# Stick-breaking attention in a four-layer trunk: from keys on partitions and softplus sums to queries on partitions, sigmoids and a reversed scan

## The chip, the cores and the metric

The kernel runs on one core of one Trainium2 chip. The core's engines each work through a queue of their own: TensorE (PE; its weight loads are listed apart as PEld), VectorE (DVE), ScalarE (ACT), GpSimd (POOL) and SyncE (SP, which issues the loads). The metric is the device time of the whole program in microseconds (us), as the median of several runs. The trace comes from one more, profiled execution.

## The reference

A trunk of four layers over 512 tokens of width 1024. Each layer is a token mixer followed by a gated FFN. The four mixers are a Conformer convolution, HGRN2, mLSTM and, in the last layer, stick-breaking attention with 16 heads of 64. Only that last mixer is touched here. What it computes for one head, with q, k, v the three thirds of `h @ w_qkv`:

```
z[i, j]  = q[i] . k[j] / sqrt(64)
log_w[i, j] = log_sigmoid(z[i, j]) + sum over l in (j, i) of log_sigmoid(-z[i, l])     for j < i
A[i, j]  = exp(log_w[i, j])   for j < i,  else 0
o[i]     = sum over j of A[i, j] v[j]
out      = concat of heads @ w_out
```

In other words, key j takes the share sigmoid(z) of what the keys between it and the query have left over; a key l leaves the share sigmoid(-z).

## The kernel before

All matrices that carry weights are multiplied as three products of high and low parts (`hh` and `hl` of the activations, `wh` and `wl` of the weights, all in the fp32r format). A weight unit of 512 KB is loaded by SP into `raw` (three buffers), ScalarE casts it to the high part (L255) and VectorE subtracts to get the low part (L257); units of an output projection are first multiplied on VectorE by the row of gates (L245). `up` (L285) makes a projection with features on partitions: 8 blocks of the input times 3 products, 24 matmuls of 512 columns for 128 features. `down` (L354) makes a projection with tokens on partitions.

`stick` (from L1149) works on 8 pairs of heads, 128 features to a pair. First the values `sv` of all heads are made, tokens on partitions, in fp32. Then, for each pair `p`, nine steps:

- `queries` and `keys`: two `up` units, `p_sqk`. From PSUM each head gets three tiles of 128 rows in which the high part stands in one half of the rows and the low part in the other (`sq`, `sk`, and `sx` with the halves exchanged), so that one matmul over 128 rows sums two of the products. ScalarE and VectorE share this work (L1211 to L1224).
- `scores`, once per head: `z`, keys on partitions and queries on columns, two fp32r matmuls for each block row (L1236). Of the 4 by 4 blocks only the 10 on and above the diagonal are made: 1280 columns in the tile `zt`, which ScalarE copies out of PSUM (L1238).
- `softplus`, once per head: Abs, Exp and Ln on ScalarE (L1247 to L1249), a VectorE step (L1250), the strict triangle on the diagonal blocks (`stri`, L1252), and the split into `sh` (ScalarE, L1253) and `sl` (VectorE, L1254).
- `weigh`, once per head: the sum over later keys is a sum over partitions, so it is done with 20 fp32r matmuls against a triangle of minus ones, `negu`, and a full square of minus ones, `negone`, into three banks `c` (L1265). VectorE adds it to `zt` (L1271), ScalarE takes Exp (L1273), VectorE clears the masked half of the diagonal blocks (`smask`, L1276).
- `mix`: values times weights in fp32, head 0 into columns 0 to 63 of the array and head 1 into 64 to 127, one bank `so` (L1284); split into `soh` and `sol` (L1287, L1288).

The steps are emitted in an order set by the table `STEPS` (a step of pair p is emitted at p plus its number) and put in place on each engine by the scheduler. Behind the last pair comes the output projection `swo`, by `down` with three units early (`pe_swo`), then the rest and the last three units (TAIL) token block by token block, so that normalisation (`X`, statistics, L581 to L626), transposes (`tr`, L512) and the new `hh` and `hl` (L517 to L524) of one token block go on beside the matmuls of the next. The FFN behind it starts with `up_head`: half the columns of three units as soon as two token blocks are ready (`p_f`).

HGRN2 uses the same program parts at its own end, but with `down_late` instead of `down`: there the last phase has 12 matmuls for each token block.

## Time and profile before

| | us |
|---|---|
| median of 3 runs | 2760.55 (2756.59 to 2761.02) |
| the profiled execution | 2756.47 |
| its span in the trace | 2754.6 |
| PE busy over the span | 2655.6 (96%) |
| DVE busy | 2027.7 (74%) |
| ACT busy | 1270.9 (46%) |
| stick-breaking from the first `p_sqk` to the first `p_f` behind it | 2141.36 to 2376.97 |

The span is what the trace covers; the 1.9 us between it and the execution's own time lie around it. Shares of busy time are means over stages with different limits, so the stage that the diff touches is read by itself in the rows below. In every PE row the duration of one matmul runs from its issue to its modelled end and overlaps its neighbours; the distance between two starts is what a matmul costs the queue. An fp32 matmul stands as two instructions in the trace, an fp32r matmul as one. A row "x16" of a timeline is 16 instructions in a row of one group, its second figure the time from the first one's start to the last one's end.

### The profile page before, as it was taken

To read this page: it belongs to the slowest core of one execution; us is meant where nothing else is said; L and a number is where in the kernel's file an instruction comes from. 1 tells how busy PE (TensorE), PEld (TensorE's weight loads), DVE (VectorE), ACT (ScalarE), POOL (GpSimd) and SP (SyncE) were. 2 spreads that over 40 slices of the span, in tenths; PEclk is the share of its full clock that TensorE was granted. 3 is DMA by queue.
4 is the path that set the end of the run, shared out by engine and by line. 5 is a ranking of instruction groups with operands and counts; after the bars stand their busy time and mean duration, and the time that the engine had idled before them with its cause. 6 is when DMAs were issued, how large, how long until landed. Compare 5 with 4: busy or idle time off the path is not lost.

```text
span 2754.6 us, 33739 instructions
## 1 busy us (share of the span) xinstructions
PE 2655.6 (96%) x12980; PEld 2128.7 (77%) x12980; DVE 2027.7 (74%) x3133; ACT 1270.9 (46%) x1773; POOL 43.7 (2%) x80
## 2 busy tenths in 40 slices
PE   7979999999998999999999999999999999999998
PEld 5538888877776788887887777888887777888886
DVE  7558997674777699667756777997676688766676
ACT  3134433345674443334545444443334798543432
POOL 0000000000000000000000000000000000000000
PEclk9989999999999999999999999999999999999999
DMA  9844874222221386232222322873333211333222
GB/s 322 235 110 155 299 236 143 95 100 89 85 72 45 126 295 222 92 102 92 98 79 77 97 79 95 276 258 121 100 103 99 62 48 31 106 100 110 97 92 77
DMA packets 109673, 352.33 MB, mean 128 GB/s; under 512 B 12104, under 2 KB 22600, under 8 KB 109512
## 3 DMA queue, kind: packets, MB, share of 16 engines
q1 hardware_dynamic: 109512, 350.17, 38.5%
q8 instruction: 102, 1.67, 0.2%
q14 instruction: 59, 0.48, 0.1%
HBM read 341.63 MB, written 8.50 MB: 127 GB/s over the span
## 4 chain that ended last, share of the span: by engine, by line
PE 79%; DVE 9%; ACT 8%; DMA 2%; issue 2%; POOL 1%; SPq 0%; POOLq 0%; DVEq 0%; ACTq 0%
PE p_f L285 34%; PE p_d L354 16%; PE p_mup L285 5%; PE p_pw L285 3%; PE p_mdn L354 3%; PE p_hqf L285 2%; PE p_hv L354 1%; PE p_sv L354 1%; PE pc L683 1%; PE p_pw L354 1%; PE p_hg L285 1%; PE p_hwo L406 1%; PE ms L977 1%; PE tr L512 1%; ACT hf L517 1%
## 5 line engine op out<-in xcount | busy, mean ns | idle before, releaser
L285 PE MATMUL p_f<-hh,wh_f 128*128 128x512 f32 (+1 forms) x1504 | 565.4, 377 | 1.5 <-ACT hh L523 1.5
L285 PE MATMUL p_f<-hl,wh_f 128*128 128x512 f32 (+1 forms) x1504 | 566.5, 377 | 0.0
L285 PE MATMUL p_f<-hh,wl_f 128*128 128x512 f32 (+1 forms) x1504 | 565.6, 376 | 0.0
L255 ACT CAST wh_f<-r_f 128x1024 fp32r<-128x1024 f32 x176 | 185.2, 1054 | 345.1 <-PE p_f L285 310.1
L285 PEld LDWEIGHTS p_f<-hh,wh_f 128*128 128x128 f32 x1504 | 284.0, 189 | 53.1 <-ACT hh L523 1.8
L285 PEld LDWEIGHTS p_f<-hl,wh_f 128*128 128x128 f32 x1504 | 284.2, 189 | 51.1 <-issue 0.2
L285 PEld LDWEIGHTS p_f<-hh,wl_f 128*128 128x128 f32 x1504 | 284.1, 189 | 51.3 <-issue 0.2
L257 DVE TENSOR_TENSOR wl_f<-r_f,wh_f 128x1024 fp32r<-128x1024 f32 x176 | 215.1, 1224 | 133.8 <-ACT wh_f L255 133.1
L211 DVE CUSTOM_DVE_ANT_0 ada<-ada,sbc,adab 128x1024 f32<-128x1024 f32 x192 | 243.9, 1280 | 6.8 <-DMA ada<-in_ada_dram 6.8
L1331 DVE SCALAR_TENSOR_TENSOR cv<-p_f,par,cv 128x511 f32<-128x511 f32 (+1 forms) x176 | 131.4, 746 | 1.4
L1331 DVE SCALAR_TENSOR_TENSOR cg<-p_f,par,cg 128x511 f32<-128x511 f32 (+1 forms) x176 | 131.3, 746 | 1.3
L245 DVE TENSOR_TENSOR r_d<-r_d,gate 128x1024 f32<-128x1024 f32 x88 | 107.5, 1222 | 28.5 <-DMA r_d<-in_fdn_dram 27.7
L1341 ACT ACTIVATE cg<-cg 128x512 f32<-128x512 f32 x88 | 55.5, 630 | 154.9 <-DVE cg L1331 154.9
L257 DVE TENSOR_TENSOR wl_d<-r_d,wh_d 128x1024 fp32r<-128x1024 f32 x88 | 107.5, 1221 | 11.7 <-ACT wh_d L255 11.7
L285 PE MATMUL p_mup<-hh,wh_mup 128*128 128x512 f32 (+1 forms) x280 | 107.4, 384 | 0.9 <-ACT hf L517 0.9
L285 PE MATMUL p_mup<-hh,wl_mup 128*128 128x512 f32 (+1 forms) x280 | 106.3, 380 | 0.0
L285 PE MATMUL p_mup<-hl,wh_mup 128*128 128x512 f32 (+1 forms) x280 | 105.9, 378 | 0.0
L255 ACT CAST wh_d<-r_d 128x1024 fp32r<-128x1024 f32 x88 | 92.4, 1050 | 20.5 <-PE p_f L285 16.6
L626 ACT ACTIVATE X<-X,mv 128x512 f32<-128x512 f32 x56 | 43.0, 811 | 79.4 <-DVE mv L614 79.4
L1329 ACT ACTIVATE cg<-p_f,par 128x512 f32<-128x512 f32 x88 | 68.2, 774 | 13.2 <-PE p_f L285 13.2
L1329 ACT ACTIVATE cv<-p_f,par 128x512 f32<-128x512 f32 x88 | 68.1, 774 | 3.9 <-PE p_f L285 3.9
L354 PE MATMUL p_d<-wl_d,gr2h 128*128 128x512 f32 x176 | 69.6, 396 | 0.0
(510 smaller groups left out, 5868.0 us busy)
## 6 DMA issues: line engine op xcount, KB each, us to landing
ada<-in_ada_dram SPq DMA_DIRECT2D x192, 512.0 KB, 4.6
r_f<-in_fup_dram SPq DMA_DIRECT2D x176, 512.0 KB, 3.9
r_d<-in_fdn_dram SPq DMA_DIRECT2D x88, 512.0 KB, 3.3
r_mup<-in_mup_dram SPq DMA_DIRECT2D x32, 512.0 KB, 3.3
r_pw<-in_pw_dram SPq DMA_DIRECT2D x24, 512.0 KB, 7.5
r_hqf<-in_hqf_dram SPq DMA_DIRECT2D x16, 512.0 KB, 3.3
r_mdn<-in_mdn_dram SPq DMA_DIRECT2D x16, 512.0 KB, 3.3
r_sqk<-in_sqk_dram SPq DMA_DIRECT2D x16, 512.0 KB, 3.6
```

The costliest lines, as they stand in the source:

```text
L211: nc.vector.tensor_tensor_reduce(out=raw, in0=raw, in1=self.sbc, scale=1.0, scalar=ab[:, j:j + 1], op0=ALU.mult, op1=ALU.add, accum_out=ac ...
L245: nc.vector.tensor_tensor(out=r, in0=r, in1=gr, op=ALU.mult)
L255: nc.scalar.copy(hi, raw)
L257: nc.vector.tensor_tensor(out=lo, in0=raw, in1=hi.bitcast(F32), op=ALU.subtract)
L285: self.nc.tensor.matmul(ps[:, c0:c1], a, b[:, k, c0:c1], start=(n == 0), stop=(n == 3 * KD - 1))
L354: self.nc.tensor.matmul(bank, l[:, ts_], r, start=(kp == first and a == n == 0), stop=(kp == last and a == 1 and n == 2))
L406: self.nc.tensor.matmul(bank, l[:, ts_], r, start=(kp == first and a == n == 0), stop=(kp == last and a == 1 and n == 2))
L512: nc.tensor.transpose(ps[:, j * P:(j + 1) * P], n[:, k * P:(k + 1) * P], self.ident)
L626: nc.scalar.activation(out=o[:, hs], in_=x[:, hs], func=AF.Identity, scale=mv[:, 2:3], bias=mv[:, 3:4])
L1329: nc.scalar.activation(out=o, in_=ps, func=AF.Identity, scale=w[2], bias=par[:, C_CONVB + m:C_CONVB + m + 1])
L1331: nc.vector.scalar_tensor_tensor(out=o[:, s:], in0=ps[:, :T - s], scalar=w[2 - s], in1=o[:, s:], op0=ALU.mult, op1=ALU.add)
L1341: nc.scalar.activation(out=cg, in_=cg, func=AF.Silu)
```

## The change

Only `stick`, its constants and one argument of `down_late` differ.

- Scores stand with queries on partitions and keys on columns. `p_sqk` is evicted once, in plain fp32, by ScalarE (tiles `sq`, `sk`, both heads in one tile). Each head's 64 rows are one row group of the array, and its matmuls are plain fp32 over 64 rows; those of the two heads alternate, into two banks. The packing into `sq`, `sk`, `sx` is gone.
- ScalarE reads each score bank twice: sigmoid(-z) into `sg` and sigmoid(z) into `sb`. The columns of one head are in two parts: 512 (query block 3) and 768 (blocks 2, 0 and 1 as 384, 128, 256).
- VectorE runs one scan over each part of `sg`, in place and from the last column to the first (multiply by `sg`, then maximum with the constant `sown`, which is 1 at the end of each block's keys and so starts the product afresh). In the rows of DVE's order below the scan stands as SCALAR_TENSOR_TENSOR. Then `sb` is multiplied by `sg` moved by one column. Softplus, the split, the `c` matmuls and Exp are gone.
- The weights now stand with queries on partitions, and `mix` wants keys there: 20 transposes of 128 by 128 for each pair (`turn_a`, `turn_c`) into banks `at`. ScalarE copies the full blocks out and VectorE masks the diagonal ones on the way (`evict`), into `sa`.
- `values` multiplies 20 blocks of 128 columns, column groups as before, into the bank `so`.
- PE's order is written by hand: a list `todo` sorted by numbers in which a pair takes 2 units. Projections go in halves of 12 matmuls between the other steps of three pairs.
- `swo` goes through `down_late`: four units early, in eight chunks of 12 matmuls, in place of the projections behind the last pair; one unit as a bridge; then 18 matmuls for each token block.
- One table of activation functions (sigmoid) is taken in place of another (ln and exp).
- SP loads the constant `sown` (128 by 896) in place of `stri` and `negu`; nothing else changes in its order.

```diff
-STEPS = dict(q0=-1.69, k0=-0.87, z0=-0.6, z1=-0.39, s0=-0.19, w0=0.2, s1=0.3, w1=0.5, m0=1.13)
-ORD = (0, 1, 3, 2)
-ZTB, SPB, SHB, SLB = 4, 2, 1, 1
+BB, AB = (2, 3), (2, 2)
...
+    dg = (p_ <= f_).astype(np.float32)
+    o["sown"] = np.concatenate([dg * x for x in (0, 0, 0, 1, 1, 0, 1)], axis=1)
...
-        hls = [[load(h, kp) for kp in left[h]] for h in range(2)]
+        last = [(h, kp) for h in range(2) for kp in left[h]][-2:]
+        hls = [[load(h, kp, spare if (h, kp) in last else None) for kp in left[h]] for h in range(2)]
...
-            self.psum(mm="01", z="237", c="456")
+            self.psum(mm="01", z="234", t="56", o="7")
...
+            W = (T, 768)
+            cols = (((3, 0),), ((2, 0), (0, 384)), ((1, 512),))
+            masks = (own[:, 0:T], own[:, P:7 * P])
...
+            def project(u, dst, half):
+                if half == 0:
...
+                    self.up_mm(st["pq"], st["hl"], 0, T, range(4))
+                    return
+                self.up_mm(st["pq"], st["hl"], 0, T, range(4, KD))
...
+                nc.scalar.copy(z, st["pq"])
...
+            def scores(p, g):
...
+                for b, c in cols[g]:
+                    w = (b + 1) * P
+                    for hh in range(2):
+                        r = slice(HD * hh, HD * hh + HD)
+                        nc.tensor.matmul(zb[hh][:, c - c0:c - c0 + w], q[r, b * P:(b + 1) * P], k[r, 0:w], start=True, stop=True,
+                                         tile_position=(HD * hh, 0))
+                    n = c - c0 + w
                 for hh in range(2):
...
+                    for name, sc in (("g", -1.0), ("b", 1.0)):
+                        nc.scalar.activation(out=st[name, p, part][hh][:, c0:c0 + n], in_=zb[hh][:, 0:n], func=AF.Sigmoid,
+                                             scale=sc * HD ** -0.5)
...
+                    nc.vector.tensor_tensor_scan(out=G[:, ::-1], data0=G[:, ::-1], data1=masks[part][:, ::-1], initial=1.0,
+                                                 op0=ALU.mult, op1=ALU.max)
+                    nc.vector.tensor_tensor(out=B[:, 0:w - 1], in0=B[:, 0:w - 1], in1=G[:, 1:w], op=ALU.mult)
+
+            def evict(ps, dst, lo, hi, dg):
+
+                nc.scalar.copy(dst[:, lo:hi], ps[:, lo:hi])
...
+                                        in1=smask.rearrange("p (a c) -> p a c", a=1).broadcast_to([P, m, P]), op=ALU.bitwise_and)
...
+                    for x in range(4):
+                        nc.tensor.transpose(ps[:, x * P:(x + 1) * P], st["b", p, part][hh][:, x * P:(x + 1) * P], self.ident)
+                    evict(ps, a[hh], 0, (384, 256)[part], (384, 256)[part])
...
+            dn = self.down_late(ins["swo"], KD, lambda k, h: so[k], "swo", done, [(1, (0, 1)), (0, (0, 1))], (2,), gate=gate,
+                                spare=lambda tag, nm: late["p"].tile([P, D], F32R, tag="tw", bufs=4, name=nm))
+            todo = []
+            for p in range(KD):
+                for z, u in (("q", p), ("k", KD + p)):
+                    for half in range(2):
+                        todo.append((2 * p + (z == "k") + half / 2, lambda u=u, d=(z, p), half=half: project(u, d, half)))
+                for at, fn in ((2.4, lambda p=p: scores(p, 0)), (2.9, lambda p=p: scores(p, 1)), (3.4, lambda p=p: scores(p, 2)),
+                               (4.4, lambda p=p: turn_a(p, 0)), (4.9, lambda p=p: values(p, (3,))), (5.4, lambda p=p: turn_a(p, 1)),
+                               (5.9, lambda p=p: turn_c(p)), (6.4, lambda p=p: values(p, (2, 0, 1)))):
+                    if p < KD - 1 or at < 6:
+                        todo.append((2 * p + at, fn))
+            for z in range(8):
+                todo.append((2 * KD + z / 2, lambda: next(dn)))
+            todo.sort(key=lambda x: x[0])
+            with tc.manual_schedule(engines={mybir.EngineType.PE}):
+                for _, fn in todo:
+                    fn()
+                values(KD - 1, (2, 0, 1))
```

PE before, in the middle of the stage: the end of a projection, the scores of head 0 of pair 2, and the first sums over later keys of head 1 of pair 1. The figures behind an underscore number the tiles.

```order
L285 MATMUL p_sqk_17426<-hh_16488,wl_sqk_17424 128x512
L1236 MATMUL z_20_17456<-sq_17215,sk_17322 128x512
L1236 MATMUL z_20_17456<-sq_17215,sx_17324 128x512
L1236 MATMUL z_20_17460<-sq_17215,sk_17322 128x384
L1236 MATMUL z_20_17460<-sq_17215,sx_17324 128x384
L1236 MATMUL z_20_17460<-sq_17215,sk_17322 128x128
L1236 MATMUL z_20_17460<-sq_17215,sx_17324 128x128
L1236 MATMUL z_20_17466<-sq_17215,sk_17322 128x256
L1236 MATMUL z_20_17466<-sq_17215,sx_17324 128x256
L1265 MATMUL c_11_17470<-sh_17408,negu 128x512
L1265 MATMUL c_11_17470<-sl_17409,negu 128x512
```

PE now, in the same place: the last values of pair 1 (query block 2, then 0, then 1), the first transposes of pair 2, and the first scores of both heads of pair 3, ahead of the next half of a projection.

```order
L281 MATMUL p_sqk_17483<-hh_16489,wl_sqk_17481 128x512
L1255 MATMUL so_17385<-sa_17427,sv_16676 64x128
L1255 MATMUL so_17385<-sa_17428,sv_16676 64x128
L1255 MATMUL so_17385<-sa_17427,sv_16674 64x128
L1255 MATMUL so_17385<-sa_17428,sv_16674 64x128
L1255 MATMUL so_17385<-sa_17469,sv_16674 64x128 x2
L1255 MATMUL so_17385<-sa_17469,sv_16675 64x128 x2
L1229 MATMUL at_20_17514<-ident,sb_17355 128x128 x4
L1229 MATMUL at_21_17521<-ident,sb_17356 128x128 x4
L1198 MATMUL z_30_17532<-sk_17467,sq_17383 128x512
L1198 MATMUL z_31_17533<-sk_17467,sq_17383 128x512
```

In one trip round the list PE now serves four pairs: it projects one, scores the one before, turns the one before that, and finishes the values of the first.

DVE before, in the middle of the stage: `sp` and `sl` are softplus and its low part, `zt` the scores that become weights.

```order
L1250 SCALAR_TENSOR_TENSOR sp_17610<-zt_17499,sp_17610 128x1280
L1222 TENSOR_TENSOR sk_17526<-p_sqk_17535,sk_17526 64x512
L1288 TENSOR_TENSOR sol_17578<-so_17568,soh_17577 128x512
L1224 CAST sx_17528<-sk_17526 64x512
L1271 TENSOR_TENSOR zt_17455<-c_20_17581,zt_17455 128x512
L1271 TENSOR_TENSOR zt_17455<-c_20_17582,zt_17455 128x512
L1271 TENSOR_TENSOR zt_17455<-c_20_17583,zt_17455 128x256
L1252 TENSOR_TENSOR sp_17610<-sp_17610,stri 128x2x128
L1252 TENSOR_TENSOR sp_17610<-sp_17610,stri 128x256
L257 TENSOR_TENSOR wl_sqk_17830<-r_sqk_17826,wh_sqk_17828 128x1024
L1276 TENSOR_TENSOR zt_17455<-zt_17455,smask 128x2x128
```

DVE now: the masks of pair 1 (`sa`, the first two of query block 2 and 0, the last of block 1) stand around the second scans and multiplications of pair 2 (`sg`, `sb`) and a weight unit.

```order
L1220 TENSOR_TENSOR sa_17427<-at_10_17429,smask 128x256
L1220 TENSOR_TENSOR sa_17428<-at_11_17436,smask 128x256
L1211 SCALAR_TENSOR_TENSOR sg_17396<-sg_17396,sown 128x768
L1211 SCALAR_TENSOR_TENSOR sg_17397<-sg_17397,sown 128x768
L1213 TENSOR_TENSOR sb_17394<-sb_17394,sg_17396 128x767
L253 TENSOR_TENSOR wl_sqk_17654<-r_sqk_17650,wh_sqk_17652 128x1024
L1213 TENSOR_TENSOR sb_17395<-sb_17395,sg_17397 128x767
L1220 TENSOR_TENSOR sa_17469<-at_1_17470,smask 128x256
```

The last row, mask of block 1, is what the `so<-sa_17469` rows of PE read; it stands on DVE behind two scans and two multiplications of the pair after it.

## Rows read from the trace of the kernel before

**Rows 1.** Busy time by stretch: the stage, one pair, HGRN2's end, the stage's end.

```profile
core 0: us, PE busy (x) PEld busy (x) DVE busy (x) ACT busy (x) POOL busy (x), PEclk, DMA share, GB/s
2141.36:2376.97 235.61, 227.72 (x1170) 180.88 (x1171) 183.82 (x270) 181.85 (x226) 1.65 (x3) 1.00 0.17 55
2256.73:2279.41 22.68, 22.09 (x122) 17.72 (x121) 20.73 (x29) 20.66 (x27) 0.00 (x0) 1.00 0.15 47
920.10:937.60 17.50, 13.80 (x66) 10.72 (x64) 15.57 (x31) 10.78 (x18) 1.12 (x2) 0.97 0.33 110
2359.50:2377.00 17.50, 16.51 (x81) 13.07 (x79) 10.65 (x27) 9.49 (x18) 1.65 (x3) 1.00 0.15 51
```

**Rows 2.** Timeline of PE, one pair: start, us, work; the wait before it in brackets.

```profile
2256.73 2.38 PE L1284 MATMUL so<-zt,sv 128*64 128x512 f32 x16
2259.03 0.50 PE L1265 MATMUL c<-sh,negu 128*128 128x512 f32 x1
...
2262.13 0.44 PE L285 MATMUL p_sqk<-hh,wh_sqk 128*128 128x512 f32 x1
...
2267.68 0.39 PE L1236 MATMUL z<-sq,sk 128*128 128x512 f32 x1
...
2268.94 0.39 PE L1265 MATMUL c<-sh,negu 128*128 128x512 f32 x1
...
2269.91 0.50 PE L1265 MATMUL c<-sl,negu 128*128 128x512 f32 x1 [0.58 <-DVE sl L1254]
...
2272.51 0.45 PE L1236 MATMUL z<-sq,sk 128*128 128x512 f32 x1
...
2273.83 0.39 PE L285 MATMUL p_sqk<-hh,wh_sqk 128*128 128x512 f32 x1
...
2279.41 1.08 PE L1284 MATMUL so<-zt,sv 128*64 128x512 f32 x4
```

**Rows 3.** Timeline of PE in HGRN2: full array, then row groups of 32.

```profile
785.76 1.16 PE L839 MATMUL hS<-QP,KP 128*128 128x128 f32 x8
786.85 1.17 PE L854 MATMUL hkv<-hv,kt 32*128 32x128 f32 x30
787.95 0.50 PE L285 MATMUL p_hqf<-hh,wh_hqf 128*128 128x512 f32 x1
```

**Rows 4.** Timeline of PE in HGRN2: four transposes and what follows.

```profile
793.53 0.60 PE L886 MATMUL hot<-ident,ob 128*128 128x128 f32 x4
793.97 1.06 PE L866 MATMUL ho<-hv,sT 128*128 128x128 f32 x8
```

**Rows 5.** DVE: scan in HGRN2; then groups by form, 2139 to 2346 (busy, mean ns).

```profile
L807 DVE TENSOR_TENSOR_SCAN B<-rst,F x8: 1218/1222/1226, 689.1 to 847.1; 128x512 f32<-128x512 f32 x8
...
L1254 DVE TENSOR_TENSOR sl<-sp,sh 128x1280 fp32r<-128x1280 f32 x16 | 23.8, 1490 | 10.6 <-ACT sh L1253 10.5
...
L1271 DVE TENSOR_TENSOR zt<-c,zt 128x512 f32<-128x512 f32 x32 | 21.4, 689 | 1.6 <-PE c L1265 1.0
...
L1276 DVE TENSOR_TENSOR zt<-zt,smask 128x256 int32<-128x256 int32 x32 | 12.1, 419 | 1.4 <-ACT zt L1273 1.3
...
L257 DVE TENSOR_TENSOR wl_sqk<-r_sqk,wh_sqk 128x1024 fp32r<-128x1024 f32 x14 | 17.1, 1220 | 15.4 <-ACT wh_sqk L255 10.0 <-PE gb L447 4.2 <-PE z L1236 1.1
```

**Rows 6.** ACT groups by form: HGRN2's sigmoid; copies and casts, 2139 to 2346.

```profile
L798 ACT ACTIVATE SG<-p_hg 128x512 f32<-128x512 f32 x8 | 4.8, 599 | 0.1
...
L1238 ACT COPY zt<-z 128x512 f32<-128x512 f32 x32 | 17.4, 583 | 0.3
...
L255 ACT CAST wh_sqk<-r_sqk 128x1024 fp32r<-128x1024 f32 x13 | 13.7, 1050 | 7.0 <-PE p_sqk L285 7.0
```

**Rows 7.** Timeline of PE at HGRN2's end: its two waits before the FFN.

```profile
934.72 1.36 PE L512 MATMUL tr<-ident,X 128*128 128x128 f32 x8 [2.14 <-ACT X L626]
...
937.63 1.01 PE L285 MATMUL p_f<-hh,wh_f 128*128 128x256 f32 x3 [1.54 <-ACT hh L523]
```

**Rows 8.** The page: DMA issues, KB each, us to landing.

```profile
r_sqk<-in_sqk_dram SPq DMA_DIRECT2D x16, 512.0 KB, 3.6
```

More of the change, by code (lines that the diff above doesn't have):

```diff
@@ L386, in down, with down_late @@
                 evict(h, t, banks[t])
-    def down_late(self, w, nk, act, name, evict, early, bridge, gate=None, rowc=None):
+    def down_late(self, w, nk, act, name, evict, early, bridge, gate=None, rowc=None, spare=None):
         npair = nk // 2
@@ L395, in down_late, with load @@
         left[0] = [kp for kp in left[0] if kp not in bridge]
-        def load(h, kp):
-            return self.unit(w, h * npair + kp, name, None if gate is None else gate[:, h * T:(h + 1) * T], rowc)
+        def load(h, kp, into=None):
+            return self.unit(w, h * npair + kp, name, None if gate is None else gate[:, h * T:(h + 1) * T], rowc, into=into)
         def mm(bank, h, t, kp, hl, first, last):
@@ L1180, in stick @@
-            free = [(kp, f"n{j}") for j in range(QKS)] + [(op, f"o{j}") for j in range(2 * KD)]
-            def slot(name, keep=False):
-                s = next(f for f in free if not keep or f[0] is op)
-                free.remove(s)
-                z = s[0].tile([P, T], F32R, tag=s[1], name=name)
-                z_slot[name] = s
-                return z
-            def drop(name):
-                s = z_slot.pop(name)
-                free.insert(sum(f[0] is kp for f in free) if s[0] is kp else len(free), s)
@@ L1278, in mix @@
-            def mix(p, av):
-                po = self.bank(f"so{p}", "z")
-                for sb in range(NT):
-                    n = T - sb * P
-                    for hh in range(2):
-                        c = (2 * p + hh) * HD
-                        nc.tensor.matmul(po[HD * hh:HD * hh + HD, sb * P:], v[sb][:, c:c + HD], av[hh][:, offs[sb]:offs[sb] + n],
-                                         start=(sb == 0), stop=(sb == NT - 1), tile_position=(0, HD * hh))
-                so.append([slot(f"so{z}{p}", True) for z in "hl"])
-                nc.scalar.copy(so[p][0], po)
-                nc.vector.tensor_tensor(out=so[p][1], in0=po, in1=so[p][0].bitcast(F32), op=ALU.subtract)
@@ new lines, in turn_a @@
+            def turn_a(p, part):
+                a = st["a", p, part] = [kp.tile([P, T], F32, tag=f"a{part}", bufs=AB[part], name=f"sa{part}{p}{hh}") for hh in range(2)]
+                for hh in range(2):
+                    ps = self.bank(f"at{part}_{p}{hh}", "t")
+                    for x in range(4):
+                        nc.tensor.transpose(ps[:, x * P:(x + 1) * P], st["b", p, part][hh][:, x * P:(x + 1) * P], self.ident)
+                    evict(ps, a[hh], 0, (384, 256)[part], (384, 256)[part])
@@ new lines, in turn_c, with values @@
+            def turn_c(p):
+                a = st["a", p, 2] = kp.tile([P, T], F32, tag="a2", bufs=1, name=f"sa2{p}")
+                ps = self.bank(f"at2_{p}", "t")
+                for x in range(2):
+                    for hh in range(2):
+                        nc.tensor.transpose(ps[:, (2 * x + hh) * P:(2 * x + hh + 1) * P],
+                                            st["b", p, 1][hh][:, 512 + x * P:512 + (x + 1) * P], self.ident)
+                evict(ps, a, 0, 256, 256)
+            def values(p, bs):
+                if ("o", p) not in st:
+                    st["o", p] = self.bank(f"so{p}", "o")
+                po = st["o", p]
+                for b in bs:
+                    for sb in range(b + 1):
+                        for hh in range(2):
+                            if b == 3:
+                                a = st["a", p, 0][hh][:, sb * P:(sb + 1) * P]
+                            elif b == 1:
+                                a = st["a", p, 2][:, (2 * sb + hh) * P:(2 * sb + hh + 1) * P]
+                            else:
+                                a = st["a", p, 1][hh][:, (3 * P if b == 0 else sb * P):][:, 0:P]
+                            c = (2 * p + hh) * HD
+                            nc.tensor.matmul(po[HD * hh:HD * hh + HD, b * P:(b + 1) * P], v[sb][:, c:c + HD], a,
+                                             start=(sb == 0), stop=(sb == b), tile_position=(0, HD * hh))
+                if 1 in bs:
+                    so.append([op.tile([P, T], F32R, name=f"so{z}{p}") for z in "hl"])
+                    nc.scalar.copy(so[p][0], po)
+                    nc.vector.tensor_tensor(out=so[p][1], in0=po, in1=so[p][0].bitcast(F32), op=ALU.subtract)
@@ L1317, in ffn @@
+            for _ in dn:
+                pass
     def ffn(self, i, nxt):
```

139 lines of the change are left out of this document (28 added, 111 removed).

## The prediction

> **What bounds the kernel now.** I read the busy time by stretch first. In the stage from the first `p_sqk` to the first `p_f` behind it PE is busy for 227.7 of 235.6 us at a granted clock of 1.00, DVE for 183.8 and ACT for 181.9 [rows 1]. PE is the bound, and what is taken from its queue comes off the end, until another engine is late. The timeline of one pair says what that queue holds [rows 2]. From one `so` to the next is 22.68 us (2256.73 to 2279.41). In it: `so` 2.30, the sums `c` of head 0 3.10, 24 `p_sqk` 5.55, `z` of head 0 1.26, `c` of head 1 3.57 with a wait of 0.58 for `sl`, `z` of head 1 1.32, the other 24 `p_sqk` 5.58. That wait is nearly all that PE loses in a pair, though DVE and ACT are busy for 20.7 of the 22.7 us [rows 1]: they are close behind. Eight pairs make 181.4 us. The 192 matmuls of `swo` at the 0.232 us that one `p_sqk` takes (5.58 / 24) make 44.5. The last 9.7 us of the stage are its two ends: the pipeline's fill, the drain of the last pair, and the normalisation that leads into the FFN.
>
> **The change, part by part, for one pair on PE.** Untouched: 48 `p_sqk`, 11.13 us. Out go both `c` with the wait for `sl` (3.10 + 3.57 = 6.67), the `z` in fp32r (2.58) and the old `so` (2.30).
>
> *Scores* are 10 blocks of 128 columns for each head, two instructions to a block. The unit price for 128 columns in fp32 is that of a transpose, (793.97 - 793.53) / 4 = 0.11 us [rows 4]; with a fresh weight load for each instruction it is 1.09 / 8 = 0.136 (`hS`, [rows 3]). The two heads sit on different rows. The nearest row is `hkv`: 32 instructions (30 recorded) on row groups of 32 in 1.10 us (786.85 to 787.95), so groups of four cost what one costs, 0.137 [rows 3]. If groups of 64 run together in the same way, scores cost 20 x 0.11 = 2.2; if not, 4.4. I take 2.2, since `hkv` is the same kind of thing and `so` does it with columns.
>
> *Values* are 20 instructions for each head, the heads on two column groups. `so` does the same 20 units of columns in 2.30, switch included [rows 2]. With 128 columns for each instruction, the price lies between 20 x 0.11 = 2.2 and 20 x 0.136 = 2.7; I take 2.2, as neighbouring tiles can load while the other computes, and keep 2.7 for the range.
>
> *Transposes* are new: 20 x 0.11 = 2.2.
>
> *Changes between the full array and tiles.* `hkv` takes 1.10 for what would be 8 x 0.11 = 0.88, and the first `p_hqf` behind it lasts 0.50 against 0.39 [rows 2, 3]: 0.22 + 0.11, about 0.35 for one trip. By `so` a trip is 0.1 (2.30 against 2.2). A pair now makes some four trips, with one change from column to row groups inside: 4 x 0.35 + 0.1 = 1.5 at the upper price, 0.5 at the lower. I take 1.5, as these trips are short. The Trainium skill (TensorEngine Tiling (Array Packing), Key Properties) says that changing the tiling mode drains TensorE. That speaks against this change, which has nine such changes in a pair; the rows agree that a trip costs something. By an estimate in which each change, and not each trip, has the 0.35 of the rows, a pair would cost 1.65 us more and the time would be 2743.
>
> PE's work for a pair: 11.13 + 2.2 + 2.2 + 2.2 + 1.5 = 19.2 us.
>
> *DVE* for a pair: scans of 2 x 512 and 2 x 768 columns. From the rows for 256 and 512 columns (0.42 and 0.69) a VectorE step has a fixed 0.15 and 1.05 ns a column; a scan of 512 takes 1.22 [rows 5], so 2.09 ns a column, and 1.76 for 768. It runs backwards and in place here, which no row shows; I take the forward price and keep twice that for a rival. Together 6.0. Multiplications of 511 and 767 columns by the rows for 512 (0.69) and 1280 (1.49) are 0.69 and 0.96 each, 3.3 for four. Masks cost 0.42 for each 256 columns: 1.8 with the single blocks. Two `wl_sqk` 2.4, `sol` 0.7. Sum 14.2, and 16.6 where `swo` units are gated: below the 20.7 of before. *ACT*: 12 sigmoids, 8 of 512 columns at 0.60 and 4 of 256 at some 0.4, 6.4; copies (0.58 for 512) 3.9, two casts 2.1: 12.4 [rows 6]. No engine other than PE is full.
>
> *The chain through DVE*, though, sets a wait, since PE's order is fixed. The masks of block 1 stand on DVE behind the second scans and multiplications of the next pair, as the order shows. Counting in one trip from the first `values` at 0, the last scores of a pair end at some 11.2. The first sigmoid comes 0.6 later (11.8), two scans of 1.76 (15.3), a multiplication (16.3), a weight unit (17.5), a multiplication (18.5) and the mask (18.9). PE, going through 24 `p_sqk` and the transposes of block 1 meanwhile, is at the values of block 1 at some 18.4 to 18.5. So it waits 0.4 to 0.5 there, and the period becomes **19.6 us** against 22.68: 3.08 for each pair, 24.6 for eight. A cheaper PE (trips at 0.1) gains little on its own, because the wait then grows: the chain is what holds it near 19.1. Queued behind that wait on PE are the transposes and scores of the following pairs, and so DVE's next scans; that is why it counts in full.
>
> *The ends.* `swo` stays at 44.5; its first 96 matmuls now fill in for projections, so that the last two pairs keep their period. At the start, one half of a projection less stands before the first scores: about 1 us is left of the fill. In the last pairs the eight partial sums into `X` (0.69 each by the row for 512) and the gated units come on DVE in front of masks: 2 us. Into the FFN, 16 transposes must be done: 1.8. And `down_late` leaves PE waiting at that point in HGRN2, 2.14 and 1.54 us, with 12 matmuls for each token block [rows 7]. Here there are 18, 4.2 us instead of 2.8, which covers 1.4 more each block, while DVE, busy for 15.6 of the 17.5 us there [rows 1], has as much to do. I take 1.5, with 0 and 3 as bounds. Ends: 1 + 2 + 1.8 + 1.5 = 6.3, against 9.7: 3.4 saved.
>
> *At no cost:* the one table of functions replaces another. `sown` is 459 KB on SP instead of 131 KB; a unit of 512 KB lands in 3.6 us [rows 8], and PE has 24 `p_sqk` before the first scan wants it, so I take 0, and 3.6 if SP's queue were late there. A word on supply: a pair in 19.6 us takes the same two units, which before came in 22.68 at a DMA share of 0.15 [rows 1].
>
> **Sum.** 24.6 + 3.4 = 28.0. On the profiled execution, 2756.47 - 28.0 = 2728.5; it lies 4.1 below the median of the runs, 2760.55, on which basis it is 2732.5. I say 2730.
>
> **The rivals.**
>
> *Heads one after the other.* If row groups of 64 don't run together, scores cost 2.2 more for a pair, 17.6 over eight: 2748. For it: no row shows 64-row groups, and the two instructions of an fp32 matmul might hold the array. Against it: `hkv` does it with four groups of 32, also in fp32. 6%.
>
> *The backwards scan is slow.* If a scan in place and backwards runs at half speed, 768 columns take 3.35 instead of 1.76 and 512 take 2.3. The chain from the last scores to the mask grows by 3.2, the period to 22.8, the sum to about 2756; DVE, then at 19.6 to 22 for a pair, also lets the partial sums and gates push the last pairs by 6 to 8 more: 2764 at worst, slower than before. It decides from 3.5 us more for each pair (28 / 8), that is, when a scan of 768 takes about 3.5. For it: each column waits for the one before, and no row shows a backwards operand. Against: HGRN2's scan is in step with its columns and nothing in it depends on direction. 6%.
>
> *DVE never late.* If sigmoids and scans start sooner than I counted (the first head's sigmoid starts before the second head's scores end) and the FFN's handover is free, the period falls to about 18.9 and the ends to 4.5: 5.6 + 1.8 less, 2721; with trips at 0.1 some 2717. For it: the wait I found is 0.5 us at the end of a chain of eight rows. 14%.
>
> *Other waits of PE.* A hand-written order has no slack: if each trip round the list has another 0.8 us of waits (a bank that ACT still reads, a weight unit that is late), eight make 6 and the time 2737. That is inside the forecast's upper half; 2737 to 2747 has 5%.
>
> *The change doesn't do what it says*: the order of the built kernel has no `c` matmul left on PE, so I set nothing aside for it.
>
> **How the numbers follow.** My forecast, a gain of 19 to 35 us with PE at 19.2 to 20.3 for a pair, has 67%. The forecast with the two cases next to it, 2715 to 2747, holds some 83%; the rival with heads apart has its price at 2748, so I draw the range from 2715 to 2748, whose upper end takes in half of it. Outside lie the slow scan, half of the heads apart, a still shorter time, and 2% for what I have not thought of. About 0.2%, 5.5 us, is what a measurement of this kernel can tell from no change. Within it: the better half of the slow scan, 3%. Slower: the worse half and what I have not thought of, 5%. Faster: the rest, 92%.
>
> **What would show it.** The distance from the `values` of one pair to those of the next, 22.68 now, should be near 19.6. Scores of the two heads should start in pairs within some hundredths of a microsecond; if they lie 0.11 apart throughout and a group of 512 columns takes 1.8 instead of 0.9, the heads don't run together. The scans should read 1.22 and 1.76. Before the last `values` of a pair PE should wait for DVE's mask, for some 0.5 us, and DVE should be busy for about 14 to 17 us in each period. At the FFN, waits on `X` and `hh` should sum to 0 to 3. The forecast is wrong if the period is above 20.5 or below 18.5, or if PE waits for a second thing in each trip round its list.

## The result and the profile after

The changed kernel takes 2731.32 us (2730.53 to 2733.84 over 4 runs) against 2760.2 before (4 runs): the ratio is 0.9899, with a 95% interval of 0.9882 to 0.9917. That is 28.9 us less, and 1.3 us from the forecast of 2730. But the sum came out right partly because two of its terms were wrong in opposite directions; the rows and experiments below say which.

The page of the profile after, and the stage, one early pair, one pair with gated units and the last but one, each from the start of its last `values` to the next pair's (columns as in [rows 1]):

```profile
span 2730.2 us, 33764 instructions
...
PE 2632.5 (96%) x13012; PEld 2101.7 (77%) x13012; DVE 1986.9 (73%) x3047; ACT 1191.4 (44%) x1749; POOL 43.7 (2%) x80
```

```profile
2143.41:2351.76 208.35, 202.61 (x1203) 151.98 (x1201) 143.13 (x184) 104.56 (x202) 1.10 (x2) 1.00 0.20 62
2208.69:2227.88 19.19, 19.19 (x125) 14.39 (x124) 13.50 (x17) 10.91 (x22) 0.00 (x0) 1.00 0.18 56
2247.08:2267.84 20.76, 19.42 (x126) 14.37 (x125) 15.74 (x20) 10.91 (x22) 0.00 (x0) 1.00 0.18 51
2288.84:2313.62 24.78, 22.29 (x135) 15.87 (x134) 18.94 (x25) 9.74 (x20) 0.00 (x0) 1.00 0.20 64
```

PE is busy for all of the 19.19 us of an early pair, where before it was busy for 22.09 of 22.68 [rows 1]. DVE has fallen from 20.73 to 13.50 and ACT from 20.66 to 10.91. The later pairs are longer, with PE idle for 1.3 us in the one and 2.5 in the other. (The last but one also holds some 3 us more of PE's work, matmuls of `swo`.)

The stage starts 3.4 us later in this execution. That need be no effect of the diff: in the traces of the first seven runs below, whose work ahead of the stage is the same, the last `p_sv` starts anywhere from 2138.2 to 2142.9. So the two kernels are best compared from the last `p_sv` to the first `p_f`. Before, then after (timelines of PE):

```profile
2137.68 0.40 PE L354 MATMUL p_sv<-wl_sv,hh 128*128 128x512 f32 x1
...
2376.73 0.52 PE L285 MATMUL p_f<-hh,wh_f 128*128 128x256 f32 x3
```

```profile
2141.07 0.40 PE L350 MATMUL p_sv<-wl_sv,hh 128*128 128x512 f32 x1
...
2351.76 0.62 PE L281 MATMUL p_f<-hh,wh_f 128*128 128x256 f32 x3
```

239.1 us became 210.7, 28.4 less: the whole gain of the medians lies in this stretch. 1.34 us of it lie ahead of the first `p_sqk`, where PE waited for `gate` before and does not now (before, then after):

```profile
2141.36 0.50 PE L285 MATMUL p_sqk<-hh,wh_sqk 128*128 128x512 f32 x1 [0.77 <-ACT gate L448]
```

```profile
2143.41 0.79 PE L281 MATMUL p_sqk<-hh,wh_sqk 128*128 128x512 f32 x1
```

Below, "the stretch" is always this one, and a run's period is the distance between the last `values` of two early pairs.

One early pair on PE, without the rows of the projections, answers to [rows 2]:

```profile
2208.69 1.53 PE L1255 MATMUL so<-sa,sv 128*64 128x128 f32 x24
2210.15 1.09 PE L1229 MATMUL at<-ident,sb 128*128 128x128 f32 x8
2211.17 1.13 PE L1198 MATMUL z<-sk,sq 64*128 64x512 f32 x4
2212.23 0.50 PE L281 MATMUL p_sqk<-hh,wh_sqk 128*128 128x512 f32 x1
...
2215.18 1.09 PE L1255 MATMUL so<-sa,sv 128*64 128x128 f32 x16
2216.20 1.14 PE L1198 MATMUL z<-sk,sq 64*128 64x384 f32 x8
...
2220.13 1.03 PE L1229 MATMUL at<-ident,sb 128*128 128x128 f32 x8
2221.09 0.70 PE L1198 MATMUL z<-sk,sq 64*128 64x256 f32 x4
...
2224.58 0.60 PE L1237 MATMUL at<-ident,sb 128*128 128x128 f32 x4
...
2227.88 1.53 PE L1255 MATMUL so<-sa,sv 128*64 128x128 f32 x24
```

There is no bracket in any of these rows: PE waits for nothing. The four `z` of 512 columns, two for each head, take 1.06 us (2211.17 to 2212.23); two alone would be 2 x 4 x 0.11 = 0.88, four in a row 1.76. So the heads run together. The new work, 20 + 20 + 20 units of 0.109, is 6.54 us, and 48 `p_sqk` 11.13; the period of 19.19 leaves 1.52 for the changes of tiling.

### The profile page after: what moved, and what is told of

The parts are those of the page before. It is cut to its first block, busy times and chain, and to the rows that moved or that the text cites. A ratio compares the mean times of both kernels' runs of the same rounds, so it can differ in the third digit from the quotient of the medians.

```text
span 2730.2 us, 33764 instructions
## 1 busy us (share of the span) xinstructions
PE 2632.5 (96%) x13012; PEld 2101.7 (77%) x13012; DVE 1986.9 (73%) x3047; ACT 1191.4 (44%) x1749; POOL 43.7 (2%) x80
## 4 chain that ended last, share of the span: by engine, by line
PE 84%; DVE 7%; ACT 4%; DMA 2%; issue 1%; POOL 1%; SPq 0%; POOLq 0%; DVEq 0%; ACTq 0%
PE p_f L281 35%; PE p_d L350 16%; PE p_mup L281 6%; PE p_pw L281 3%; PE p_mdn L350 3%; PE p_sqk L281 2%; PE p_hqf L281 2%; PE p_hg L281 1%; PE p_hv L350 1%; PE p_sv L350 1%; PE p_pw L350 1%; PE pc L680 1%; PE p_hwo L402 1%; PE ms L974 1%; PE tr L509 1%
```

## Experiments

Each kernel is the changed one with the edit shown, shortened to what differs. Ratios are to the kernel before, as in the result. Stretch and period come from one trace for each run.

| run | ratio (95% interval) | median us | stretch us | period us |
|---|---|---|---|---|
| the change | 0.9899 (0.9882 to 0.9917) | 2731.3 | 210.7 | 19.19 |
| heads apart | 0.9960 (0.9945 to 0.9975) | 2747.3 | 225.8 | 22.05 |
| no gates | 0.9878 (0.9863 to 0.9892) | 2724.6 | 206.4 | 19.19 |
| one scan more | 0.9940 (0.9924 to 0.9957) | 2742.5 | 224.0 | 20.9 |
| block 1 early | 0.9919 (0.9905 to 0.9934) | 2736.3 | 216.1 | 19.31 |
| old `down` | 0.9907 (0.9892 to 0.9922) | 2732.5 | 211.3 | 19.19 |
| gates on POOL | 0.9924 (0.9910 to 0.9939) | 2737.0 | 217.3 | 19.19 |
| POOL, block 1 early | 0.9903 (0.9886 to 0.9919) | 2731.6 | 212.4 | 19.31 |
| sums first | 0.9893 (0.9878 to 0.9908) | 2729.9 | 210.1 | 19.19 |
| POOL, block 1, sums first | 0.9888 (0.9873 to 0.9902) | 2727.2 | 206.1 | 19.31 |
| block 1, sums first | 0.9903 (0.9886 to 0.9919) | 2731.6 | 210.3 | 19.31 |
| the same, fewer changes | 0.9909 (0.9894 to 0.9924) | 2733.9 | 212.0 | 19.0 |
| POOL and all | 0.9878 (0.9861 to 0.9894) | 2726.3 | 204.3 | 19.0 |

Only the intervals of "heads apart" and "one scan more" lie clear of that of the change. What is said of the other runs rests on their rows.

My theory after the result: PE's own rows set the early pairs; DVE's chain to the last mask is only just in time; what the last pairs lose, they lose to DVE's queue. Rival theories: DVE's chain, not PE, sets every pair; or the late pairs lose to loads.

### Heads apart

```diff
-((2.4, lambda p=p: scores(p, 0)), (2.9, lambda p=p: scores(p, 1)), (3.4, lambda p=p: scores(p, 2)),
+((2.39, lambda p=p: scores(p, 0, 0)), (2.4, lambda p=p: scores(p, 0, 1)),
+ (2.89, lambda p=p: scores(p, 1, 0)), (2.9, lambda p=p: scores(p, 1, 1)),
+ (3.39, lambda p=p: scores(p, 2, 0)), (3.4, lambda p=p: scores(p, 2, 1)),
```

> The change, but the two heads' score matmuls are put apart: head 0's stand ahead of the values or transposes of their place in PE's list, head 1's behind them, so that the two row groups can't run together. If the row groups are worth what the trace shows (partners start 7 ns apart), each pair pays the 20 instructions of 0.11 us again, 2.2 us, and some 0.4 for two or three more changes of tiling: the period goes from 19.2 to about 21.8 us, the time to some 2731 + 8 x 2.6 = 2752. If PE's rows are not what sets the period (DVE's chain to the last mask is), part of it is hidden, and the time stays below 2742.

The timeline of PE, where the heads of one score part now stand on either side of the values:

```profile
2220.30 1.13 PE L1198 MATMUL z<-sk,sq 64*128 64x384 f32 x4
2221.36 1.09 PE L1255 MATMUL so<-sa,sv 128*64 128x128 f32 x16
2222.38 1.13 PE L1198 MATMUL z<-sk,sq 64*128 64x384 f32 x4
```

One head's 512 columns now take 1.06 us, what both heads took together (2216.20 and its x8 above). The period is 22.05, 2.86 more, where 2.6 was expected: 2.2 of matmuls and 0.66 for four changes of tiling more (13 in a pair instead of nine). The time rose by 16 us, which lies between the two cases, and the stretch by 15.1. In the first pair nothing stands between the heads, and there they still run together:

```profile
2155.75 1.13 PE L1198 MATMUL z<-sk,sq 64*128 64x512 f32 x4
```

So seven pairs pay, 7 x 2.86 = 20.0. Most of the rest is waits that are no longer there: with PE slower, the masks and partial sums of the last pairs come nearly in time, and all waits of PE in the stretch add up to 4.2 us less; of those for masks and sums only one of 0.2 us is left. So the row groups are worth their full 2.2 us in an early pair, where PE is the bound, and less at the end, where DVE is late. The same gain on PE was worth less where the other engine was late.

### No gates

```diff
-dn = self.down_late(ins["swo"], ..., (2,), gate=gate,
+dn = self.down_late(ins["swo"], ..., (2,), gate=None,
```

> The change, with the output projection's weights not multiplied by the row of gates (that part of the computation is left out), so that eight VectorE steps of 1.22 us are gone. If the two waits of PE for a mask (1.5 and 1.1 us above a matmul's own distance, at 2248 and 2269) come from these steps standing in DVE's queue, both go and every pair has the period 19.2: about 2728, a little less if the waits on the partial sums shrink too. If they come from a late load, or from something else in the last pairs, they stay: 2731.

The waits to explain stand in the changed kernel's timeline like this (PE, the first pair with gated units):

```profile
2247.08 1.31 PE L1255 MATMUL so<-sa,sv 128*64 128x128 f32 x20
2249.73 0.44 PE L1255 MATMUL so<-sa,sv 128*64 128x128 f32 x4 [1.34 <-DVE sa L1220]
```

and this is DVE ahead of that mask:

```profile
2241.29 1.23 DVE L241 TENSOR_TENSOR r_swo<-r_swo,gate 128x1024 f32<-128x1024 f32 x1 [4.04 <-DMA r_swo<-in_swo_dram]
2242.43 0.75 DVE L1220 TENSOR_TENSOR sa<-at,smask 128x256 int32<-128x256 int32 x2
2243.10 3.40 DVE L1211 TENSOR_TENSOR_SCAN sg<-sg,sown 128x768 f32<-128x768 f32 x2
2246.41 0.93 DVE L1213 TENSOR_TENSOR sb<-sb,sg 128x767 f32<-128x767 f32 x1
2247.26 1.22 DVE L253 TENSOR_TENSOR wl_sqk<-r_sqk,wh_sqk 128x1024 fp32r<-128x1024 f32 x1
2248.39 0.95 DVE L1213 TENSOR_TENSOR sb<-sb,sg 128x767 f32<-128x767 f32 x1
2249.26 0.42 DVE L1220 TENSOR_TENSOR sa<-at,smask 128x256 int32<-128x256 int32 x1
```

The gated unit stands ahead of the masks in DVE's order, and DVE stood idle for 4 us ahead of it, because its load had not landed. SP issued that load only when DVE's last step on a weight unit was done (2236.03 + 1.22) and its buffer free:

```profile
2237.27 0.33 SPq L236 DMA_DIRECT2D r_swo<-in_swo_dram  x1
```

So the masks start 14.55 us behind their pair's values (2227.88 to 2242.43). Without the gates it is 12.48, from 2226.65:

```profile
2239.13 0.86 DVE L1220 TENSOR_TENSOR sa<-at,smask 128x256 int32<-128x256 int32 x2 [3.12 <-ACT sa L1217]
```

Of the 2.07 us between the two, 1.14 are the gated step and 0.93 its wait for the load. Without the gates the same place of PE shows one row without a wait, and four periods in a row are 19.19, where the change has three:

```profile
2265.04 1.53 PE L1255 MATMUL so<-sa,sv 128*64 128x128 f32 x24
```

The time fell by 6.7 us, 4.3 of it in the stretch, more than the 2.3 of the two masks. The period of the last but one pair fell too, from 24.78 to 23.44, although one wait on a partial sum (1.0) stayed. So the late masks come from the gated step in DVE's order. But the run takes away the step and its wait for the load together, and the load had a share in the delay. A unit loaded earlier would have fitted into the 4 us in which DVE was idle; no run tries that, and how much of the loss an earlier load would give back stays open.

### One scan more

```diff
+if part == 1 and hh == 0:
+    junk = kp.tile([P, 768], F32, ...)
+    nc.vector.tensor_tensor_scan(out=junk[:, ::-1], data0=G[:, ::-1], data1=masks[part][:, ::-1], ...)
```

> The change, with one more scan of 768 columns on DVE for each pair, into a scrap tile, ahead of the two that count. DVE is busy for some 14 of 19.2 us in a pair. If the mask of block 1 is just in time, as the rows read (it ends at 2228.84, the matmuls ahead of its readers at about 2228.8), the 1.76 us count in full in seven pairs: a period of 20.9 and about 2731 + 12 = 2743. If DVE's idle time took it up, the time stays at 2731; a half price would put the slack at 0.9 us.

```profile
2212.24 1.31 PE L1258 MATMUL so<-sa,sv 128*64 128x128 f32 x20
2215.03 0.44 PE L1258 MATMUL so<-sa,sv 128*64 128x128 f32 x4 [1.48 <-DVE sa L1223]
```

One scan of 1.76 us more lengthens the period by 1.7, from 19.19 to 20.9, though DVE was idle for almost 6 us of a pair. The wait appears exactly where the prediction had put it. The time, 2742.5, is that of the first case. The slack was at most 0.1 us, so the chain is just in time. A scan at half speed (3.2 us more in the chain) would by the same price have cost what the rival of the slow scan said, a gain near zero; no run has such a scan.

### Block 1 early

```diff
-(5.9, lambda p=p: turn_c(p))
+(4.9, lambda p=p: turn_c(p))
```

> The change, with the transposes of block 1 moved from 5.9 to 4.9 in the list, so that the mask of block 1 stands on DVE ahead of the scans of the next pair. If the steady period is PE's own work, it stays at 19.2 (less some 0.1 for a trip saved), while the two waits behind gated units go: 2.6 us less, and 2727 to 2729 in all. If the two banks for transposes become the next wait (the one of block 1 must be free again within one half of a projection), the period grows, and the time is above 2733.

The theory on the pairs was right, and its time was missed. The early pairs and the first gated one have 19.31, with no wait for a mask in the values. This is what decides between PE and DVE's chain: with the mask of block 1 ahead of the scans the chain has slack, and the period still stays. It went up by 0.12, not down, because the transposes now stand between two tilings instead of between projections, which makes ten changes of tiling instead of nine. The second case named the time (above 2733), but the banks for transposes cost only one wait of 0.95 us (at 2281.99). What was gained came back with interest behind the last scores:

```profile
2302.59 0.50 PE L402 MATMUL pe_swo<-wh_swo,soh 128*128 128x512 f32 x1 [4.12 <-DVE X L578]
...
2316.20 0.51 PE L402 MATMUL p_swo<-wl_swo,soh 128*128 128x512 f32 x1 [1.94 <-DVE wl_swo L253]
```

The last but one period is 33.39 us instead of 24.78. PE comes to the second half of the early `swo` sooner, and needs two banks that the partial sums into `X` must free first; on DVE these stand behind a gated unit and two scans with their multiplications. A wait was moved, not removed.

### Old `down`

```diff
-dn = self.down_late(ins["swo"], KD, lambda k, h: so[k], "swo", done, ...
...
-for z in range(8):
-    todo.append((2 * KD + z / 2, lambda: next(dn)))
...
+self.down(ins["swo"], KD, lambda k, h: so[k], "swo", 2, evict, tail=TAIL, gate=gate,
+          early=3, ...
```

> The change without its last part: behind the pairs the output projection goes as before, with three units early and three at the end, instead of standing in PE's list. Theory: in the changed kernel 96 of its matmuls are what PE works on while the last pairs go through ACT and DVE; without them PE has no projection left there, and waits for some 8 to 12 us of the chain from the last scores to the last values, of which the scheduler can fill a part with the early units. 2736 to 2741. If the early units fill the gap as well as the list does, or the time lost to waits on partial sums in the list is as large as what it covers, the time stays within 3 us of 2731.

The second case: 2732.5, and the intervals overlap. The scheduler put the early units between the last pairs' steps by itself; the waits for masks add to 4.5 us there, against 2.3 in the changed kernel, and those for partial sums are gone. That part of the change is worth nothing that these runs can tell.

### Gates on POOL

```diff
-nc.vector.tensor_tensor(out=r, in0=r, in1=gr, op=ALU.mult)
+(nc.gpsimd if name == "swo" else nc.vector).tensor_tensor(out=r, in0=r, in1=gr, op=ALU.mult)
```

> The change, with the output projection's weights multiplied by the gates on POOL instead of DVE; nothing is left out. POOL is idle there; no trace shows it on a tile of 128 by 1024, so its price is open. Theory: DVE's queue loses the eight steps of 1.22 us, as in the run without gates, and that run's time comes back, 2725 to 2727. If POOL is slow enough that a unit comes late (each is wanted some 11 us after the one before it), or if DVE's own steps get longer while POOL works, the gain is lost: 2731 or more.

Slower by 5.7 us than the change (the intervals overlap; the stretch is 6.6 us longer). POOL, and DVE beside it:

```profile
2238.21 2.40 POOL L241 TENSOR_TENSOR r_swo<-r_swo,gate 128x1024 f32<-128x1024 f32 x1 [139.56 <-DMA r_swo<-in_swo_dram]
```

```profile
2238.53 5.34 DVE L1211 TENSOR_TENSOR_SCAN sg<-sg,sown 128x768 f32<-128x768 f32 x2 [0.21 <-ACT sg L1203]
```

Two scans take 5.34 us where they took 3.41 in the changed kernel. The 1.93 more is nearly what POOL still had to do when they started (2238.21 + 2.40 - 2238.53 = 2.08). So by these rows DVE all but stood still while POOL worked, and the step of 1.22 us was exchanged for a stop of 2. The Trainium skill (SBUF — State Buffer, Who interferes with whom) says that a DVE step with both inputs in SBUF contends with a POOL step that reads SBUF, and that the shared port pair is an exclusive lock. The rows agree with it. 5.6 us of the loss lie in the last but one pair (30.42 us instead of 24.78), where PE waits 4.2 us for partial sums instead of 1.9.

### Three combinations

The first has the edits of the two runs "gates on POOL" and "block 1 early" together.

> Gates on POOL and the transposes of block 1 early. The run with the transposes early alone kept 19.31 us in every pair, but lost 4.1 us to partial sums and 1.9 to a weight's low part behind the last scores. Theory: those two were late because DVE's order had the gated units and four scans ahead of them; without the gates at least half of it goes, and the time is 2726 to 2730. If the loss comes from the order of the scans alone, it stays near 2733.

The pairs kept 19.31, and PE no longer waits for a partial sum. But the time, 2731.6, lies between the two cases: PE waited 4.4 us for a low part of a `swo` unit behind the last scores, and the last but one period was 29.97.

"Sums first" raises the priority of the partial sums on DVE:

```diff
+if spare:
+    hp.enter_context(self.tc.high_priority(offset=XPRIO))
 for t in range(2):
     evict(h, t0 + t, banks[t], True)
```

> The change, with one thing else: the partial sums of the output projection come ahead of the scans in DVE's order. Theory: the waits of PE on partial sums behind the last scores (1.1 and 1.3 us above a matmul's distance, at 2298 and 2308) go, and the masks still wait in the two pairs with gated units (2.6 us): 2728 to 2730. If the sums in front of the last scans push the masks of the last pairs back by as much, the time stays at 2731.

2729.9, at the upper edge of the first case, and its interval overlaps with that of the change, so the run does not decide between the two. Of the waits on partial sums one of 0.7 us is left. The last but one period went from 24.78 to 21.19, but 2.5 us of it came back in the last (15.84 instead of 13.36), and PE still waits 3.5 us for masks in four places.

The third has gates on POOL, block 1 early and sums first together.

> Gates on POOL, transposes of block 1 early, and the partial sums of the output projection ahead of the scans in DVE's order. Theory: what PE waits for behind the last scores are the two banks that a partial sum on DVE has to free; with the sums first those waits go, the last but one pair comes near 20 us where the changed kernel has 24.8, and the time is 2721 to 2725. If the last pair's scans, which now stand behind, become the wait, there is no gain over the run before: 2726 to 2730.

2727.2 is 4.4 us less than the same without sums first, but it lies in the second case and not in the 2721 to 2725 of the first. In the rows the first case's mechanism is there: the last but one period is 21.07, and of the waits on partial sums 0.9 us is left. Scans still met POOL (mean 2.09 us for the 16 of 768 columns, 1.74 in the change).

### The same without POOL, and fewer changes of tiling

> Transposes of block 1 early and partial sums first, the gates on DVE as in the change. In the run with the gates on POOL as well, each scan that met POOL was longer (mean 2.09 instead of 1.76 us for 768 columns) and the period of the last pairs was 19.67 and 21.08. Theory: without POOL the DVE steps have their own length again and the gated units fit into DVE's idle time, since no mask waits behind them any more: the pairs keep 19.3, the last but one some 21, and the time is 2723 to 2727. If the gated units again come ahead of the last partial sums, nothing is gained over the run with POOL: 2727 or more.

The second case: 2731.6. Four periods are 19.31, and behind the last scores PE waits 3.0 us for a partial sum: in the order of DVE a gated unit and two scans stand ahead of the first sum.

```diff
-(2.4, lambda p=p: scores(p, 0)), ... (4.9, lambda p=p: turn_c(p)), (6.4, lambda p=p: values(p, (2, 0, 1)))
+(2.46, lambda p=p: scores(p, 0)), ... (4.85, lambda p=p: turn_c(p)), (6.45, lambda p=p: values(p, (2, 0, 1)))
```

> The run before, with PE's list in another order: transposes ahead of values in two places, so that the full array's fp32 transposes follow the full array's fp32r matmuls, and two of the nine changes of tiling in a pair are gone. Theory: a change costs about 0.1 us of PE (a matmul behind one starts 0.20 after the last, instead of 0.11): the period goes from 19.3 to 19.1 and the time is 1.6 us less. If a change costs 0.35 us, the period goes to 18.6 and the time is 5 us less. If it costs nothing, or another wait takes its place, the period stays.

Two changes of tiling fewer (eight instead of ten) bring the period from 19.31 to 19.0: 0.15 us for each, between the two prices that I had put up. The time did not follow. It rose, within the intervals, since another wait came in: values of block 3 now follow those of the pair before so soon that the single bank `so` is not yet free (waits of PE, the largest row):

```profile
PE so L1259 <- DVE sol L1264: 6.2, 3, 3.0
```

> The fastest run so far (gates on POOL, transposes of block 1 early, partial sums first) with PE's list in the order of the run with two changes of tiling fewer. There the steady period was 18.99 instead of 19.31, but PE waited up to 3 us for the low part of the mixed values, with a gated unit in front of it on DVE. Theory: with the gates on POOL that wait is small, the shorter period counts in six or seven pairs, and the time is some 2 us below 2727: 2724 to 2726. If the low part is still late, because POOL makes DVE's steps longer, the time is 2727 or more.

2726.3, with the shortest stretch of all, 204.3 us. The first case's 2724 to 2726 was just missed by the median. Its 0.9878 (0.9861 to 0.9894) still overlaps with the 0.9899 of the change and is no proof by itself; but its stretch is 6.4 us shorter and the medians say 5.0.

Each of the three kernels with POOL and block 1 early is faster than its partner with the gates on DVE: 2731.6 against 2736.3, 2727.2 against 2731.6, 2726.3 against 2733.9. The intervals of the first two pairs overlap, those of the third just touch. So POOL is not a wrong place as such. That its stop costs only while a mask stands behind the scans fits these three kernels, in which no row of PE waits for a mask; no run shows it by itself.

## Why the prediction was right, and where it was not

**PE's work for a pair: right.** 19.2 us was forecast, 19.19 measured. Scores at 2.2, values at the lower price, transposes at 0.11 and 1.5 for the changes of tiling all stand in the rows. The account behind the 1.5 was wrong in kind, though, and that its sum came out is luck. I priced four trips of 0.35 and treated a change inside a trip as 0.1. What the runs fit is a price for each change: 1.52 / 9 = 0.17 in the changed kernel, 0.15 by the run with two fewer, 0.12 by the one with one more (block 1 early), and 0.66 / 4 = 0.17 by the one with four more. The Trainium skill (TensorEngine Tiling (Array Packing), Key Properties) says that changing the tiling mode drains TensorE. Counting by changes, as it does, is the better description, though no row shows a drain as such; the estimate of 0.35 for each that I put beside it was twice too high.

**The wait in the chain: wrong, 0.4 to 0.5 us forecast, none there.** I had the place and the order right, and added up durations. Consecutive DVE steps overlap at their ends: from the scans at 2222.24 to the mask at 2228.42 are 6.18 us of start to start, while the durations that I added up for these five steps are 1.76 x 2 + 0.96 + 1.22 + 0.96 = 6.66.

```profile
2222.24 3.41 DVE L1211 TENSOR_TENSOR_SCAN sg<-sg,sown 128x768 f32<-128x768 f32 x2 [0.22 <-ACT sg L1203]
2225.57 0.94 DVE L1213 TENSOR_TENSOR sb<-sb,sg 128x767 f32<-128x767 f32 x1
2226.41 1.22 DVE L253 TENSOR_TENSOR wl_sqk<-r_sqk,wh_sqk 128x1024 fp32r<-128x1024 f32 x1
2227.55 0.96 DVE L1213 TENSOR_TENSOR sb<-sb,sg 128x767 f32<-128x767 f32 x1
2228.42 0.42 DVE L1220 TENSOR_TENSOR sa<-at,smask 128x256 int32<-128x256 int32 x1
```

The half microsecond of wait was this overlap. The mask ends at 2228.84, and its first reader on PE stands behind 20 of the 24 instructions of that row (as the waits above show), two heads at a time, so it could start at 2227.88 + 10 x 0.11 = 2228.98: just in time. At that period eight pairs save 8 x 3.49 = 27.9 us and not 24.6; what the later pairs lose is counted under the ends.

**The ends: wrong the other way.** 3.4 us of gain were forecast. Of the 28.4 us of the stretch, 27.9 are the pairs' and 1.34 lie ahead of the first `p_sqk`, which the forecast had not counted at all. So in the forecast's own stage the ends became 0.9 us longer. (The first `p_f` before starts at 2376.73, not at the 2376.97 of the table and of [rows 1].) Two terms failed. For the partial sums and gated units in front of masks I had 2 us. The waits in those pairs add up to 5.0: 1.34 and 0.97 for masks, 0.93 and 0.98 for partial sums, 0.47 and 0.31 for ACT (the 1.34 is shown above).

```profile
2270.12 0.44 PE L1255 MATMUL so<-sa,sv 128*64 128x128 f32 x4 [0.97 <-DVE sa L1220]
...
2287.24 0.50 PE L402 MATMUL pe_swo<-wh_swo,soh 128*128 128x512 f32 x1 [0.31 <-ACT sk L1182]
...
2298.78 0.50 PE L402 MATMUL pe_swo<-wh_swo,soh 128*128 128x512 f32 x1 [0.93 <-DVE X L578]
...
2307.22 0.50 PE L402 MATMUL p_swo<-wh_swo,soh 128*128 128x512 f32 x1 [0.47 <-ACT wh_swo L251]
...
2309.42 0.50 PE L402 MATMUL pe_swo<-wh_swo,soh 128*128 128x512 f32 x1 [0.98 <-DVE X L578]
```

I had counted lateness in front of masks only. With two banks for the early `swo`, each partial sum is itself something that PE waits for. And `swo` did not stay at 44.5: from start to start and without the waits its 192 matmuls take 47.3 us (45.9 before, by the same count). Against that, the 1 us set aside for the fill was not needed: from the first `p_sqk` to the mask at 2249.73 PE has no wait.

That the sum met the time is luck: the pairs saved 3.3 us more than forecast, the ends 4.3 less, and 1.3 came from a place that the forecast left out.

**The handover into the FFN: right.** 1.5 us forecast with 0 to 3 as bounds; 0.55 for `X` and 0.73 for `hl` measured, against 2.14 and 1.54 in HGRN2 [rows 7].

```profile
2341.32 0.66 PE L509 MATMUL tr<-ident,X 128*128 128x128 f32 x4 [0.55 <-ACT X L623]
...
2353.11 0.38 PE L281 MATMUL p_f<-hl,wh_f 128*128 128x256 f32 x1 [0.73 <-DVE hl L521]
```

**The scan: right.** Backwards and in place, it has the forward price (1.22 for 512 columns in [rows 5], and 1.76 was worked out for 768):

```profile
L1211 DVE TENSOR_TENSOR_SCAN sg<-sg,sown x32: 1198/1477/1758, 2159.3 to 2306.2; 128x512 f32<-128x512 f32 x16, 128x768 f32<-128x768 f32 x16
```

**The rivals.** Heads one after the other did not happen; made to happen, it cost 16 us and would have brought 2747 where the rival said 2748. That nearness is partly chance: the run also pays for four changes of tiling in a pair that the rival did not have, one pair of the eight was not touched, and waits at the end went away. The slow scan did not happen; a dose of it showed the price, 1.7 us of period for 1.76 of scan. Other waits of PE, a second one in each trip, did not come in the early pairs; the last four have 5.0 us in all. "DVE never late" was true of the early pairs and untrue of the last. PE was the bound, as read; the gain is what left its queue, and it is fully seen only where no other engine is late.

## What to carry to other kernels

Count what a change takes from the queue of the bounding engine row by row, and every change of tiling in it; then look at each place of a fixed order for what is queued on the other engine in front of the step that it reads. Idle time on that engine need be no slack: DVE was idle for almost a third of a pair, and yet one step more of 1.76 us cost 1.7. And where a chain of short steps decides, add up their distances from start to start, not their durations.

## What the runs showed of the hardware that was not expected

- Matmuls of two row groups of 64 in fp32 run together in full: 512 columns of both heads in 1.06 us, of one head alone in 1.06 as well.
- A change of tiling cost PE 0.12 to 0.17 us on average, by four runs with eight to 13 changes in a pair. Straight from column to row groups it was no dearer than to the full array: 16 `so` and the change to `z` took 1.02 us (2215.18 to 2216.20), 0.15 above 8 x 0.109; 24 `so` and the change to `at` 1.46 (2208.69 to 2210.15), 0.15 above 12 x 0.109. The order of a list of small groups was worth some 0.3 us in a pair of 19.
- A VectorE scan of 768 columns stopped for nearly as long as a POOL multiplication still ran: two took 5.34 us instead of 3.41 beside the last 2.08 us of one on POOL. Though POOL was idle for 98% of the span, moving a step of 1.22 us there made the changed kernel 5.7 us slower; with block 1 early the same move made it 4.4 to 7.6 us faster.
